# Second FF product by seven quarter products: three sweeps in place of two, and stores on GpSimd's queue

## The chip, the core and the metric

One NeuronCore of a Trainium2 chip runs the whole program. The metric is the device time of one execution in microseconds (us). Three runs of the kernel before gave 828.68, 830.63 and 832.57 us, a median of 830.63. Engines are named TensorE (PE, with PEld for its weight loads), VectorE (DVE), ScalarE (ACT), GpSimd (POOL) and SyncE (SP, which only issues DMAs here).

## The reference, cut to what matters

The program is a decoder block for 512 tokens of width 1024 in float32: gated attention and convolution mixers, a projection with norm and residual, and then a squared-ReLU MLP. The change touches the last part alone:

```python
def squared_relu_mlp(h, w_ff1, w_ff2):
    return jnp.square(jax.nn.relu(h @ w_ff1)) @ w_ff2
...
    f = squared_relu_mlp(rms_norm(x, norm_mlp_pre[l]), w_ff1[l], w_ff2[l])
    x = x + rms_norm(f, norm_mlp_post[l])
```

Here h is 512 x 1024, w_ff1 is 1024 x 4096 and w_ff2 is 4096 x 1024.

## The kernel before, in words

Every float32 operand of a matmul is split into a high part (a cast to float32r on ScalarE) and a low part (the difference, on VectorE), and `mm3` (lines 84 to 88) issues three matmuls per product: high x high, high x low, low x high. A matmul has a 128x128 stationary block and 512 moving columns.

The first FF product works through 32 blocks j of 128 FF channels. `wsplit` (99) loads a block's weights in two halves into `raw` buffers (tag `raw`, six of them, `NRAW`), casts them into `whi` and subtracts into `wlo` (four each), and `ff1_part` (685) runs 24 matmuls into a PSUM bank. `ff1_end` (694) takes the ReLU on ScalarE and the product with the bank on VectorE; the result, FF channels by tokens, stays in `f1`. Two blocks, j = 2p and 2p + 1, make a pair p; there are 16 pairs (`NP`).

The second FF product sums, over the pairs, products of 2 x 2 blocks: the rows are the lower and the upper token half (256 tokens), the columns of w_ff2 are its two halves of 512, and the inner index is the pair's two blocks. Instead of eight quarter products it takes seven (Strassen's scheme in Winograd's form), of two token tiles and three matmuls each: 42 matmuls for a pair. PSUM has eight banks of 128x512, and a quarter product needs two for as long as it is summed over the pairs, so the seven are made in two sweeps over the pairs. The names in the code: a for the quarters of `f1`, b for those of w_ff2, s and t for sums of them.

- The first sweep runs along with the first FF product. For each pair `first_operands` (737) loads the four quarters of w_ff2 (`quarter`, 720, into `raw` buffers), forms the sums s2, s3, t3, t2, t4, splits them, and overwrites quarters of `f1` with the sums that the second sweep needs. `first_sweep` (757) of pair p - 1 follows, three quarter products in six banks, 18 matmuls: s3 t3, s2 t2, a22 t4.
- The second sweep has four quarter products (`second_operands`, 762; `second_products`, 779), 24 matmuls for a pair. It loads all four quarters of w_ff2 again, forms t1 again and splits the whole of `f1[p]`. The first product of pair 0 is placed ahead of the last step of the first sweep, since two banks are free by then.
- The end (834 to 854) takes the last two pairs (`TAIL`) token tile by token tile and product by product. As banks are completed, VectorE combines them into output tiles: tiles 2 and 3 (lower half) from products 0 and 1 and the sums `g` and `h` of the first sweep, tiles 0 and 1 from products 2 and 3 and `e`. `post` (827) takes the mean square (`square_sums`, 643: ScalarE squares with a sum, GpSimd adds and raises to -0.5), multiplies by the gain, adds the residual and stores (`finish`, 820), all stores on SP's queue.

Who goes when: the program is written in order, but a planner of the language sets the order on each engine and queue beforehand, by its own estimates of costs and by the program's order as priority; a tile is given one of its tag's buffers when one is free. On the chip each engine works its list in order and waits where an operand or a buffer is not ready. SP's list holds the loads and, before the change, the output stores.

Of the kernel before, what the change touches and what calls it, by code (L numbers as in the profile page):

```python
# [11 lines left out]
F32 = mybir.dt.float32  # L12
F32R = mybir.dt.float32r
# [6 lines left out]
P = 128  # L20
# [26 lines left out]
NRAW = 6  # L47
# [11 lines left out]
def decoder_block(ctx: ExitStack, tc: tile.TileContext, a: dict, out: bass.AP):  # L59
# [15 lines left out]
    def stile(name, dt=F32):  # L75
        return spool.tile([P, 512], dt, tag="s", name=name, bufs=6)
# [657 lines left out]
    def htile(name, dt=F32R):  # L734
        return hpool.tile([P, 4, S], dt, tag="h", name=name, bufs=4)

    def first_operands(p):

        f = f1[p]
        b12, b22, b11, b21 = (quarter(2 * p + r, c) for r, c in ((0, 1), (1, 1), (0, 0), (1, 0)))  # L740
        w = [htile(f"x{x}{p}") for x in "hl"]
        s23 = stile(f"s23{p}")
        a22 = stile(f"a22{p}", F32R)
        split(a22[:, half[0]], a22[:, half[1]], f[:, 1, half[1]])
        dve.tensor_tensor(s23[:, half[1]], f[:, 0, half[0]], f[:, 0, half[1]], ALU.subtract)
        dve.tensor_tensor(f[:, 0, half[1]], f[:, 0, half[1]], f[:, 1, half[1]], ALU.add)
        dve.tensor_tensor(s23[:, half[0]], f[:, 0, half[1]], f[:, 0, half[0]], ALU.subtract)
        split(w[0][:, 3, :], w[1][:, 3, :], s23)
        ts = [stile(f"t{n}{p}") for n in (3, 2, 4)]
# [12 lines left out]
    def second_operands(p):  # L762

        b12, b11, b21, b22 = (quarter(2 * p + r, c, *t) for r, c, *t in (
            (0, 1, "whi", NSPLIT), (0, 0), (1, 0), (1, 1)))
        t1 = stage.tile([P, 512], F32, tag="wlo", name=f"t1{p}", bufs=NSPLIT)
        l = htile(f"l{p}")
        w = [r3.tile([P, 4, 512], F32R, tag="sw", name=f"y{x}{p}", bufs=4) for x in "hl"]
        split(l[:, 0:2, :], l[:, 2:4, :], f1[p])
        split(w[0][:, 0, :], w[1][:, 0, :], b11)  # L770
        dve.tensor_tensor(t1, b12, b11, ALU.subtract)
        for n, src in ((1, t1), (2, b21), (3, b22)):
            split(w[0][:, n, :], w[1][:, n, :], src)
        return l, w


    LEFT = ((0, 0), (0, 1), (1, 0), (1, 1))

    def second_products(p, ops, which, toks=(0, 1)):
        l, w = ops  # L780
        for n in which:
            r, c = LEFT[n]
            products(bcc[n], [l[:, r, half[c]], l[:, 2 + r, half[c]]], [x[:, n, :] for x in w], p == 0, p == NP - 1, toks)

    ops = {}
    for p in range(NP):
        for j in (2 * p, 2 * p + 1):
            if j < BRIDGE:
                pf, w = early[j]
                ff1_part(pf, w, SPLIT, S)  # L790
            else:
                w = wsplit(a["w_ff1"][j], f"f1{j}", eng=dve)
                pf = ps(f"pf{j}")
                ff1_part(pf, w, 0, S)
            ff1_end(j, pf)
        ops[p] = first_operands(p)
        if p == 1:
            acc = [[scs(f"p70"), scs("p71")], [cvtile("p60"), cvtile("p61")], [tps("p40"), ps("p41")]]
        if p:
            first_sweep(p - 1, ops.pop(p - 1))  # L800
    gout = gain("g_out", a["norm_mlp_post"], D)
    second = second_operands(0)
    bcc = [[ps(f"p1{t}") for t in range(2)]]
    second_products(0, second, (0,))
    first_sweep(NP - 1, ops.pop(NP - 1))

    e, g = (ratile(n) for n in ("e", "g"))
    h = wtile("h")
    for t in range(2):
        act.copy(e[:, t, :], acc[1][t])  # L810
        dve.tensor_tensor(g[:, t, :], acc[0][t], e[:, t, :], ALU.add)
        dve.tensor_tensor(h[:, t, :], g[:, t, :], acc[2][t], ALU.subtract)
    bcc += [[cvtile(f"p5{t}") for t in range(2)], [scs(f"p2{t}") for t in range(2)], [tps("p30"), ps("p31")]]
    second_products(0, second, (1, 2, 3))
    for p in range(1, NP - TAIL):
        second_products(p, second_operands(p), range(4))

    o_ = [wtile(f"o{t}") for t in range(NT)]

    def finish(t, r):  # L820
        for c, n in ((0, 512), (512, 512)) if t != 1 else ((0, 512), (512, 256), (768, 256)):
            hf, c1 = divmod(c, 512)
            piece = o_[t][:, hf, c1:c1 + n]
            dve.scalar_tensor_tensor(piece, piece, r, x1[t][hf][:, c1:c1 + n], ALU.mult, ALU.add)  # L824
            sp.dma_start(out[t * P:(t + 1) * P, c:c + n], piece)

    def post(t):
        src = [o_[t][:, hf, :] for hf in range(2)]
        r = square_sums(src, f"o{t}")
        for hf in range(2):  # L830
            dve.tensor_tensor(src[hf], src[hf], gout[:, hf * 512:(hf + 1) * 512], ALU.mult)  # L831
        finish(t, r)

    last = [(p, second_operands(p)) for p in range(NP - TAIL, NP)]
    for t in range(2):
        v = stile(f"v{t}")
        for n in (0, 1, 2, 3):
            for p, x in last:
                second_products(p, x, (n,), (t,))
            bank = bcc[n][t]  # L840
            if n == 0:
                act.copy(v, bank)
                dve.tensor_tensor(o_[t + 2][:, 0, :], v, h[:, t, :], ALU.add)
            elif n == 1:
                dve.tensor_tensor(g[:, t, :], g[:, t, :], bank, ALU.add)
                dve.tensor_tensor(e[:, t, :], e[:, t, :], bank, ALU.add)  # L846
                dve.tensor_tensor(o_[t + 2][:, 1, :], g[:, t, :], v, ALU.add)
                post(t + 2)
                pool.tensor_tensor(e[:, t, :], e[:, t, :], v, ALU.add)  # L849
            elif n == 2:  # L850
                dve.tensor_tensor(o_[t][:, 0, :], v, bank, ALU.add)
            else:
                dve.tensor_tensor(o_[t][:, 1, :], e[:, t, :], bank, ALU.add)
                post(t)


def _layout(i):
# [58 lines left out]
```

## Time and profile before

| | before |
|---|---|
| median of three runs | 830.63 us |
| the profiled execution | 830.19 us, of which its span 828.4 |
| TensorE busy | 797.4 us, 96% of the span |
| VectorE, ScalarE, GpSimd busy | 633.0, 419.7, 215.6 us |
| TensorE's granted clock, mean | 0.991 of full |
| DMA queue of SP and the other hardware queues, GpSimd's | 94.09 and 1.57 MB |
| bytes read from and written to HBM | 93.54 and 2.10 MB |

The profile is of one execution. Times in it count from the start of the span. "Busy" sums the instructions of an engine; a matmul's shown end is modelled, and matmuls overlap, so that one with 0.40 us shown can be followed by the next after 0.23. In a timeline an arrow names what ended the idle time before an instruction. SPq and POOLq are the instructions that issue a DMA on these engines' queues; the time to landing counts from the issue until all bytes are there.

### The profile page before, as it was taken

The numbers are of one execution on the slowest core, as the hardware profiler recorded it, in microseconds if no ns is written. First come the engines' busy times: TensorE is split into PE (matmuls) and PEld (weight loads), VectorE is DVE, ScalarE is ACT, GpSimd is POOL, SyncE is SP. The second block draws the span as 40 slices with busy tenths as digits, with TensorE's granted clock in tenths as the row PEclk, the third lists the DMA queues.
The fourth block names the chain that finished last, engine by engine and source line by source line (L and its number), as shares of the span: only waits on it lengthen the run. The fifth ranks groups of instructions, "written<-read, shape, count | busy, mean of one in ns | idle before, by whom it ended". The sixth has DMA issues, their size and how long they took to land. (4 is left out here: it accounts for less than half of the span.)

```text
span 828.4 us, 11002 instructions
## 1 busy us (share of the span) xinstructions
PE 797.4 (96%) x3786; PEld 660.7 (80%) x3786; DVE 633.0 (76%) x1046; ACT 419.7 (51%) x792; POOL 215.6 (26%) x203
## 2 busy tenths in 40 slices
PE   8989999999999999899999999999999999999992
PEld 8967888888888887687878898888888888788871
DVE  5689999999999996596573547857657657798777
ACT  6667775867673233365442324434334334555642
POOL 3244433433434645648711100000000000000003
PEclk9999999999999999999999999999999999999997
DMA  8412121122112223245450014544434334466422
GB/s 265 137 41 90 52 80 51 53 80 70 68 62 100 91 101 104 89 162 188 159 191 1 27 49 155 178 135 144 141 127 153 128 127 165 154 210 202 157 67 101
DMA packets 54344, 96.36 MB, mean 116 GB/s; under 512 B 6288, under 2 KB 11280, under 8 KB 54288
## 3 DMA queue, kind: packets, MB, share of 16 engines
q1 hardware_dynamic: 53856, 94.09, 34.1%
q0 software_dynamic: 432, 1.57, 0.5%
q8 instruction: 30, 0.49, 0.3%
q14 instruction: 26, 0.21, 0.1%
HBM read 93.54 MB, written 2.10 MB: 115 GB/s over the span
## 5 line engine op out<-in xcount | busy, mean ns | idle before, releaser
L559 DVE SCALAR_TENSOR_TENSOR cv<-u,convw,cv 128x512 f32<-128x512 f32 x232 | 161.9, 747 | 0.2
L87 PE MATMUL pf<-h2l,whi_f 128*128 128x512 f32 (+1 forms) x256 | 97.4, 380 | 0.0
L86 PE MATMUL pf<-h2h,whi_f 128*128 128x512 f32 (+1 forms) x256 | 97.3, 380 | 0.0
L88 PE MATMUL pf<-h2h,wlo_f 128*128 128x512 f32 (+1 forms) x256 | 97.3, 381 | 0.0
L112 DVE TENSOR_TENSOR wlo_f<-raw_f,whi_f 128x512 fp32r<-128x512 f32 x60 | 41.1, 690 | 65.1 <-ACT whi_f L111 63.9
L849 POOL TENSOR_TENSOR e<-e,v 128x512 f32<-128x512 f32 x2 | 3.2, 1600 | 329.4 <-DVE e L846 329.4
L111 ACT CAST whi_f<-raw_f 128x512 fp32r<-128x512 f32 x60 | 36.9, 621 | 85.0 <-PE pf L87 50.0
L112 POOL TENSOR_TENSOR wlo_gt<-raw_gt,whi_gt 128x512 fp32r<-128x512 f32 x32 | 43.9, 1374 | 50.1 <-ACT whi_gt L111 50.1
L87 PEld LDWEIGHTS pf<-h2l,whi_f 128*128 128x128 f32 x256 | 48.2, 188 | 9.9
L86 PEld LDWEIGHTS pf<-h2h,whi_f 128*128 128x128 f32 x256 | 48.2, 188 | 9.9
L88 PEld LDWEIGHTS pf<-h2h,wlo_f 128*128 128x128 f32 x256 | 48.2, 188 | 9.8
L86 PE MATMUL pg<-hTh,whi_gt 128*128 128x512 f32 x128 | 51.4, 402 | 0.0
L88 PE MATMUL pg<-hTh,wlo_gt 128*128 128x512 f32 x128 | 50.6, 396 | 0.0
L87 PE MATMUL pg<-hTl,whi_gt 128*128 128x512 f32 x128 | 50.5, 395 | 0.0
L86 PE MATMUL p<-yh,l 128*128 128x512 f32 x128 | 50.4, 395 | 0.0
L87 PE MATMUL p<-yl,l 128*128 128x512 f32 x128 | 50.4, 395 | 0.0
L88 PE MATMUL p<-yh,l 128*128 128x512 f32 x128 | 50.2, 395 | 0.0
L726 ACT CAST yh<-f 128x512 fp32r<-128x512 f32 x48 | 28.0, 617 | 36.8 <-PE p L87 27.6
L727 DVE TENSOR_TENSOR yl<-f,yh 128x512 fp32r<-128x512 f32 x48 | 31.7, 687 | 14.8 <-ACT yh L726 14.7
L111 ACT CAST whi_gt<-raw_gt 128x512 fp32r<-128x512 f32 x32 | 19.8, 618 | 40.1 <-PE pg L87 37.0
L726 ACT CAST xh<-t 128x512 fp32r<-128x512 f32 x48 | 29.6, 619 | 19.5 <-DVE t L751 19.5
L727 DVE TENSOR_TENSOR xl<-t,xh 128x512 fp32r<-128x512 f32 x48 | 31.5, 684 | 0.5 <-ACT xh L726 0.5
(314 smaller groups left out, 2278.6 us busy)
## 6 DMA issues: line engine op xcount, KB each, us to landing
f<-in_w_ff SPq DMA_DIRECT2D x128, 256.0 KB, 3.0
raw_f<-in_w_ff SPq DMA_DIRECT2D x64, 256.0 KB, 3.0
raw_gt<-in_w_zm SPq DMA_DIRECT2D x32, 256.0 KB, 2.5
raw_gb<-in_w_zm SPq DMA_DIRECT2D x16, 256.0 KB, 2.6
raw_ga<-in_w_zm SPq DMA_DIRECT2D x16, 256.0 KB, 2.6
raw_wo<-in_w_o SPq DMA_DIRECT2D x16, 256.0 KB, 2.6
raw_pw<-in_w_pw SPq DMA_DIRECT2D x16, 256.0 KB, 2.7
raw_wout<-in_w_out SPq DMA_DIRECT2D x16, 256.0 KB, 2.7
```

The source lines that it names most:

```text
L86: pe.matmul(o, lhsT=lh, rhs=rh, start=first, stop=False)
L87: pe.matmul(o, lhsT=lh, rhs=rl, start=False, stop=False)
L88: return pe.matmul(o, lhsT=ll, rhs=rh, start=False, stop=last)
L111: recent[act] = act.copy(hi, raw)
L112: recent[e] = e.tensor_tensor(lo, raw, f32(hi), ALU.subtract)
L559: dve.scalar_tensor_tensor(co[j] if tap == CW - 1 else acc[j], src, convw[:, i, tap:tap + 1], acc[j], ALU.mult, ALU.add)
L726: act.copy(hi, src)
L727: dve.tensor_tensor(lo, src, f32(hi), ALU.subtract)
L849: pool.tensor_tensor(e[:, t, :], e[:, t, :], v, ALU.add)
```

## The change

- The seven products are made in three sweeps. The first, still along with the first FF product, has a11 b11, s2 t2 and s3 t3. The second has two products that complete the lower token half (they read the upper columns of `f1[p]`, and t1 and t4). The third has two that complete the upper half (with b21 and b22 raw from w_ff2).
- t1 and t4 are formed in the first sweep, in place in the `raw` buffers of b12 and b21, and stored to DRAM (`keep`), 32 stores of 256 KB on GpSimd's queue; the second sweep loads them back into `whi` and `raw` buffers instead of two quarters of w_ff2.
- `later_operands` splits half of `f1[p]` (512 columns) for each of the later sweeps, and two right operands.
- Ahead of the first sweep's last step stand the first products of pairs 0 and 1 of the second sweep.
- `lower` is a generator of 14 steps that finishes output tiles 2 and 3; one step is taken behind each pair 0 to 13 of the third sweep. Their stores go to GpSimd's queue, those of tiles 0 and 1 stay on SP's.
- The last two pairs of the third sweep are taken token tile by token tile, as before, with two products each; one VectorE addition completes an output half.

```diff
+    def keep(name, p, src):
+        kept[name, p] = dram.tile([P, 512], F32, tag=f"{name}{p}", name=f"{name}{p}")
+        pool.dma_start(kept[name, p], src)
...
     def first_operands(p):
...
-        a22 = stile(f"a22{p}", F32R)
-        split(a22[:, half[0]], a22[:, half[1]], f[:, 1, half[1]])
+        a11 = stile(f"a11{p}", F32R)
+        split(a11[:, half[0]], a11[:, half[1]], f[:, 0, half[0]])
+        split(w[0][:, 0, :], w[1][:, 0, :], b11)
...
-        ts = [stile(f"t{n}{p}") for n in (3, 2, 4)]
-        for n, (t, x, y, op) in enumerate(((ts[0], b22, b12, ALU.subtract), (ts[1], ts[0], b11, ALU.add), (ts[2], ts[1], b21, ALU.subtract))):
-            dve.tensor_tensor(t, x, y, op)
-            split(w[0][:, n, :], w[1][:, n, :], t)
-        dve.tensor_tensor(f[:, 1, half[1]], f[:, 1, half[0]], s23[:, half[0]], ALU.subtract)
+        t3, t2 = (stile(f"t{n}{p}") for n in (3, 2))
+        dve.tensor_tensor(t3, b22, b12, ALU.subtract)
+        dve.tensor_tensor(t2, t3, b11, ALU.add)
+        split(w[0][:, 2, :], w[1][:, 2, :], t3)
+        split(w[0][:, 1, :], w[1][:, 1, :], t2)
+        dve.tensor_tensor(b12, b12, b11, ALU.subtract)
+        keep("t1", p, b12)
+        dve.tensor_tensor(b21, t2, b21, ALU.subtract)
+        keep("t4", p, b21)
+        dve.tensor_tensor(f[:, 0, half[0]], f[:, 1, half[0]], s23[:, half[0]], ALU.subtract)
         s2, s3 = ([x[:, 3, h] for x in w] for h in half)
-        return (s3, s2, [a22[:, h] for h in half]), w
+        return ([a11[:, h] for h in half], s2, s3), w
...
+    def later_operands(p, beta):
+
+        if beta:
+            raw = [quarter(2 * p + 1, c) for c in range(2)]
+        else:
+            raw = []
+            for n, (tag, bufs) in (("t1", ("whi", NSPLIT)), ("t4", ("raw", NRAW))):
+                raw.append(stage.tile([P, 512], F32, tag=tag, name=f"{n}b{p}", bufs=bufs))
+                sp.dma_start(raw[-1], kept[n, p])
...
+        w = r3.tile([P, 4, 512], F32R, tag="sw", name=f"y{beta}{p}", bufs=4)
+        split(l[:, 0:2, :], l[:, 2:4, :], f1[p][:, :, half[1 - beta]])
+        for n in range(2):
+            split(w[:, n, :], w[:, 2 + n, :], raw[n])
         return l, w
...
+    ahead = [later_operands(p, 0) for p in range(2)]
+    bcc = [[ps(f"p5{t}") for t in range(2)]]
+    for p in range(2):
+        later_products(p, 0, ahead[p], (0,))
     first_sweep(NP - 1, ops.pop(NP - 1))
...
+    for t in range(2):
+        act.copy(u1[:, t, :], acc[0][t])
+    for t in range(2):
+        dve.tensor_tensor(u2[:, t, :], acc[1][t], u1[:, t, :], ALU.add)
+        dve.tensor_tensor(u3[:, t, :], acc[2][t], u2[:, t, :], ALU.add)
...
+    for p in range(2):
+        later_products(p, 0, ahead[p], (1,))
+    for p in range(2, NP):
+        later_products(p, 0, later_operands(p, 0))
...
+            (sp if t < 2 else pool).dma_start(out[t * P:(t + 1) * P, c:c + n], piece)
+            yield
...
+    def lower():
+        for t in range(2):
+            yield from post(t + 2, (
+                lambda: dve.tensor_tensor(o_[t + 2][:, 0, :], u3[:, t, :], bcc[1][t], ALU.subtract),
+                lambda: dve.tensor_tensor(o_[t + 2][:, 1, :], u3[:, t, :], bcc[0][t], ALU.add),
+                lambda: dve.tensor_tensor(u2[:, t, :], u2[:, t, :], bcc[0][t], ALU.add)))
+
+    rest = lower()
+    for p in range(NP - TAIL):
+        later_products(p, 1, later_operands(p, 1))
+        next(rest, None)
+    last = [(p, later_operands(p, 1)) for p in range(NP - TAIL, NP)]
+    for _ in rest:
+        pass
+    upper = [post(t, ()) for t in range(2)]
     for t in range(2):
+        for n, src in ((0, u1), (1, u2)):
             for p, x in last:
+                later_products(p, 1, x, (n,), (t,))
+            dve.tensor_tensor(o_[t][:, n, :], src[:, t, :], bcc[2 + n][t], ALU.add)
+            if t and n == 0:
+                next(upper[0])
+                next(upper[0])
+    for u in upper:
+        for _ in u:
+            pass
```

## Rows read from the trace of the kernel before

**Rows 1.** Page, part 1: busy us (share) xinstructions of each engine

```profile
PE 797.4 (96%) x3786; PEld 660.7 (80%) x3786; DVE 633.0 (76%) x1046; ACT 419.7 (51%) x792; POOL 215.6 (26%) x203
```

**Rows 2.** Stretches: us; busy PE, PEld, DVE, ACT, POOL; PEclk, DMA share, GB/s

```profile
670.00:700.00 30.00, 30.00 (x131) 24.39 (x131) 19.17 (x37) 12.32 (x22) 0.00 (x0) 1.00 0.41 140
700.00:720.00 20.00, 18.02 (x79) 14.35 (x78) 14.13 (x27) 9.68 (x18) 0.00 (x0) 1.00 0.60 198
740.00:760.00 20.00, 20.00 (x87) 16.11 (x86) 17.71 (x25) 11.58 (x19) 0.00 (x0) 1.00 0.63 208
800.00:828.40 28.40, 12.10 (x52) 9.20 (x50) 22.38 (x33) 9.01 (x22) 8.20 (x10) 0.79 0.20 74
```

**Rows 3.** Timeline at the seam: start, duration, instruction, [idle before it <-releaser]

```profile
712.65 0.69 DVE L699 TENSOR_TENSOR f<-pf,rl 128x512 f32<-128x512 f32 x1 [1.15 <-ACT rl L696]
...
715.65 0.40 PE L88 MATMUL p<-xh,a 128*128 128x512 f32 x1
...
715.80 0.62 ACT L726 CAST yh<-f 128x512 fp32r<-128x512 f32 x1 [1.72 <-DMA f<-in_w_ff]
...
716.33 1.13 ACT L726 CAST xh<-t 128x512 fp32r<-128x512 f32 x2
...
718.03 0.73 PE L86 MATMUL p<-xh 128*128 128x512 f32 x2 [1.98 <-ACT xh L726]
```

**Rows 4.** Timeline of the tail

```profile
811.70 0.40 PE L88 MATMUL p<-yh,l 128*128 128x512 f32 x1
...
820.62 0.67 DVE L853 TENSOR_TENSOR o<-e,p 128x512 f32<-128x512 f32 x1
...
821.38 0.63 ACT L647 ACTIVATE j_o<-o 128x512 bf16<-128x512 f32 x1 [1.80 <-DVE o L853]
...
823.08 0.56 POOL L145 TENSOR_TENSOR r_o<-v_o,mhalf 128x1 f32<-128x1 f32 x1
...
823.67 1.54 DVE L824 SCALAR_TENSOR_TENSOR o<-o,r_o,x 128x512 f32<-128x512 f32 x3 [0.85 <-POOL r_o L145]
```

**Rows 5.** Groups by shape, 720 to 800: busy us, mean ns | idle

```profile
L727 DVE TENSOR_TENSOR l<-f,l 128x1024 fp32r<-128x1024 f32 x16 | 19.5, 1222 | 0.1
...
L771 DVE TENSOR_TENSOR t<-f,f 128x512 f32<-128x512 f32 x15 | 10.3, 685 | 1.9 <-DMA f<-in_w_ff 1.8
```

**Rows 6.** Timeline of pairs 0 and 1 in the first sweep

```profile
493.46 0.42 DVE L745 TENSOR_TENSOR s<-f 128x256 f32<-128x256 f32 x1
...
495.07 0.68 DVE L751 TENSOR_TENSOR t<-t,f 128x512 f32<-128x512 f32 x1
...
495.78 7.08 SPq L104 DMA_DIRECT2D raw_f<-in_w_ff  x4
...
498.84 0.62 ACT L111 CAST whi_f<-raw_f 128x512 fp32r<-128x512 f32 x1 [0.26 <-DMA raw_f<-in_w_ff]
...
499.02 0.42 DVE L753 TENSOR_TENSOR f<-f,s 128x256 f32<-128x256 f32 x1
...
500.55 0.68 DVE L112 TENSOR_TENSOR wlo_f<-raw_f,whi_f 128x512 fp32r<-128x512 f32 x1
...
501.94 0.39 PE L86 MATMUL pf<-h2h,whi_f 128*128 128x512 f32 x1
```

**Rows 7.** DMA issues: xcount, KB each, median us from issue to landing

```profile
f<-in_w_ff SPq DMA_DIRECT2D x128, 256.0 KB, 3.0
...
out<-o SPq DMA_DIRECT2D x7, 256.0 KB, 2.0
...
g_out<-in_norm_mlp_post POOLq DMA_DIRECT2D x1, 512.0 KB, 4.0
```

**Rows 8.** Timeline of POOL: the last DMA issue on its queue

```profile
475.86 0.64 POOL L140 DMA_DIRECT2D g_out<-in_norm_mlp_post  x1
```

**Rows 9.** Timeline at block 30: first cast of its weights, first use

```profile
689.42 0.62 ACT L111 CAST whi_f<-raw_f 128x512 fp32r<-128x512 f32 x1 [2.34 <-DMA raw_f<-in_w_ff]
...
700.61 0.39 PE L86 MATMUL pf<-h2h,whi_f 128*128 128x512 f32 x1
```

More of the change, by code (lines that the diff above doesn't have):

```diff
@@ L735, in htile @@
         return hpool.tile([P, 4, S], dt, tag="h", name=name, bufs=4)
+    dram = open_pool(ctx, "dram", bass.MemoryType.DRAM)
+    kept = {}
+    def keep(name, p, src):
+        kept[name, p] = dram.tile([P, 512], F32, tag=f"{name}{p}", name=f"{name}{p}")
+        pool.dma_start(kept[name, p], src)
     def first_operands(p):
@@ L760, in first_sweep, with later_products @@
             products(bank, l, [x[:, n, :] for x in w], p == 0, p == NP - 1)
[L762 to L773, printed above, removed]
+    lpair = [None]
+    def later_operands(p, beta):
[6 more added lines that the diff above has]
+                sp.dma_start(raw[-1], kept[n, p])
+        if not beta and p < 2:
+            l = rapool.tile([P, 4, 2 * P], F32R, tag="ra", name=f"l{beta}{p}", bufs=4)
+        else:
+            if p % 2 == 0:
+                lpair[0] = hpool.tile([P, 8, 2 * P], F32R, tag="h", name=f"l{beta}{p}", bufs=4)
+            l = lpair[0][:, 4 * (p % 2):4 * (p % 2) + 4, :]
+        w = r3.tile([P, 4, 512], F32R, tag="sw", name=f"y{beta}{p}", bufs=4)
+        split(l[:, 0:2, :], l[:, 2:4, :], f1[p][:, :, half[1 - beta]])
+        for n in range(2):
+            split(w[:, n, :], w[:, 2 + n, :], raw[n])
         return l, w
-    LEFT = ((0, 0), (0, 1), (1, 0), (1, 1))
-    def second_products(p, ops, which, toks=(0, 1)):
+    def later_products(p, beta, ops, which=(0, 1), toks=(0, 1)):
         l, w = ops
         for n in which:
-            r, c = LEFT[n]
-            products(bcc[n], [l[:, r, half[c]], l[:, 2 + r, half[c]]], [x[:, n, :] for x in w], p == 0, p == NP - 1, toks)
+            r = 1 - n if beta else n
+            products(bcc[2 * beta + n], [l[:, r, :], l[:, 2 + r, :]], [w[:, n, :], w[:, 2 + n, :]],
+                     p == 0, p == NP - 1, toks)
     ops = {}
@@ L797, in decoder_block @@
         if p == 1:
-            acc = [[scs(f"p70"), scs("p71")], [cvtile("p60"), cvtile("p61")], [tps("p40"), ps("p41")]]
+            acc = [[scs("p10"), scs("p11")], [cvtile("p60"), cvtile("p61")], [tps("p70"), ps("p71")]]
         if p:
@@ L801, in decoder_block, with post @@
     gout = gain("g_out", a["norm_mlp_post"], D)
-    second = second_operands(0)
-    bcc = [[ps(f"p1{t}") for t in range(2)]]
-    second_products(0, second, (0,))
+    ahead = [later_operands(p, 0) for p in range(2)]
+    bcc = [[ps(f"p5{t}") for t in range(2)]]
+    for p in range(2):
+        later_products(p, 0, ahead[p], (0,))
     first_sweep(NP - 1, ops.pop(NP - 1))
-    e, g = (ratile(n) for n in ("e", "g"))
-    h = wtile("h")
+    u12, u3 = htile("u12", F32), htile("u3", F32)
+    u1, u2 = u12[:, 0:2, :], u12[:, 2:4, :]
     for t in range(2):
[L810 to L816, printed above, removed]
-    o_ = [wtile(f"o{t}") for t in range(NT)]
-    def finish(t, r):
+        act.copy(u1[:, t, :], acc[0][t])
+    for t in range(2):
+        dve.tensor_tensor(u2[:, t, :], acc[1][t], u1[:, t, :], ALU.add)
+        dve.tensor_tensor(u3[:, t, :], acc[2][t], u2[:, t, :], ALU.add)
+    bcc += [[f(f"{n}{t}") for t in range(2)] for f, n in ((scs, "p4"), (cvtile, "p2"))] + [[tps("p30"), ps("p31")]]
+    for p in range(2):
+        later_products(p, 0, ahead[p], (1,))
+    for p in range(2, NP):
+        later_products(p, 0, later_operands(p, 0))
+    o_ = [wtile(f"o{t}") for t in range(NT)]
+    def post(t, combine):
+        src = [o_[t][:, hf, :] for hf in range(2)]
+        for c in combine:
+            c()
+            yield
+        r = square_sums(src, f"o{t}")
+        for hf in range(2):
+            dve.tensor_tensor(src[hf], src[hf], gout[:, hf * 512:(hf + 1) * 512], ALU.mult)
+            yield
         for c, n in ((0, 512), (512, 512)) if t != 1 else ((0, 512), (512, 256), (768, 256)):
@@ L824, in finish @@
             dve.scalar_tensor_tensor(piece, piece, r, x1[t][hf][:, c1:c1 + n], ALU.mult, ALU.add)
[L825 to L834, printed above, removed]
+            (sp if t < 2 else pool).dma_start(out[t * P:(t + 1) * P, c:c + n], piece)
@@ new lines, in post @@
+            yield
+    def lower():
[8 more added lines that the diff above has]
+        next(rest, None)
@@ L835, in decoder_block @@
+    last = [(p, later_operands(p, 1)) for p in range(NP - TAIL, NP)]
+    for _ in rest:
+        pass
+    upper = [post(t, ()) for t in range(2)]
     for t in range(2):
-        v = stile(f"v{t}")
-        for n in (0, 1, 2, 3):
+        for n, src in ((0, u1), (1, u2)):
             for p, x in last:
[L839 to L854, printed above, removed]
+                later_products(p, 1, x, (n,), (t,))
[3 more added lines that the diff above has]
+                next(upper[0])
```

## The prediction

> **What bounds the kernel now.** I read the page's first part, then the busy time by stretches, then the timeline at the two places where TensorE is not full. TensorE is busy for 797.4 of the 828.4 us span [rows 1]. By stretches it is full (30.00 of 30) in the first sweep and full in the second, at a granted clock of 1.00, with 87 matmuls in 20 us, or 0.230 us each; it loses 2 us around 716 and most of the stretch after 800 [rows 2]. So a saving can come from three things only: fewer matmuls, the gap at the seam between the sweeps, or the tail. The matmuls stay the same: 7 products of 6 matmuls per pair of FF blocks, 42, before and after (18 + 24 now, 18 + 12 + 12 then).
>
> The seam [rows 3]: the last matmul of sweep 14 starts at 715.65, and the next, the first of pair 15, at 718.03, after 1.98 us idle. It waited for ScalarE's cast of t3. ScalarE could not make it: the cast ahead of it in its queue, an operand of the second sweep, sat until 715.80 for a load of w_ff2 (1.72 us idle). The casts that TensorE needed followed at 716.33.
>
> The tail [rows 4]: the last matmul starts at 811.70 and takes 0.40, so TensorE ends at 812.10 and the span 16.3 us later. VectorE then works off both halves of token tile t=1: combinations, squares, gains, residuals, stores. The last combination starts only at 820.62, and what follows it is a chain to the end: ScalarE's square (821.38), GpSimd's power (823.08), the three residual pieces (823.67 to 825.21), the store and the end of the program at 828.4, 7.78 us in all.
>
> **The change, part by part.**
>
> *Tail.* The four lower output halves are finished during the third sweep: 14 steps of one VectorE instruction, one behind each of the pairs 0 to 13. After the last matmul there is one combination of t=1 (I allow 0.1 us between them), then the same chain of 7.78 us. In that chain VectorE also has two residual pieces of t=0 (1.4) and two gain products (1.3); with the combination these 3.4 us fit before GpSimd's power, due 3.0 us after the combination began, almost exactly. So 7.9 us in place of 16.3: **-8.4 us**. If the planner puts t=0's two pieces ahead of the last combination, 1.5 us come back; below 7.8 it cannot go.
>
> What hides the 14 steps: a pair in the third sweep takes TensorE 12 x 0.230 = 2.76 us. VectorE has one half-width left operand (512 columns, 0.69 by the 512-column row; the full one takes 1.222), two low parts (2 x 0.69) and the step (0.69) [rows 5], 2.74 us. That looks like no margin, but back to back such instructions start every 0.60 us (seven of 512 and four of 256 columns start between 493.46 and 499.02) [rows 6], so 2.4 us, and operands lie up to four pairs ahead (four `sw` buffers). I take zero, with 1 us as the upper end. The first step waits for the last bank of the second sweep; behind it on VectorE wait the operands of pair 1, for which there are 2.76 us and 2.4 are needed: zero.
>
> *Seam.* Sweep 15 now begins with a11 b11, which needs neither t3 nor s3, and the second sweep's filler ahead of it is 12 matmuls instead of 6 (pairs 0 and 1, from kept tiles). After the first matmul block ends, TensorE has sweep 14 (18), the filler (12) and a11 b11 (6): 36 x 0.230 = 8.3 us, to about 720.2. The operands of s2 t2 follow f (712.65 to 713.34) by two half sums, two sums, three casts and low parts, some 4 us, thus by 717.5. The wait goes: **-2.0 us**. Late next would be the left operand of pair 2, whose buffer comes free when sweep 15 ends; the n=1 products of pairs 0 and 1 (12, 2.76 us) cover its cast and low part (1.3) and VectorE's two u3 sums (1.3). Bounds: -2.2 to 0.
>
> *Loads and stores.* The second and third sweep load two quarters each per pair, four together as now; in the third all use the six `raw` buffers, three pairs or 8.3 us deep, against a load of 3.0 us [rows 7] and some 2 us of cast and subtraction: zero. New are 32 stores of 256 KB during the first sweep. On GpSimd, busy 0.00 there [rows 2], one issue takes 0.64 us [rows 8], so 20 us on an idle engine; behind them on its queue is nothing that TensorE needs. On the DMA engines the stores add two transfers to eight per pair: 0.41 of their time [rows 2] becomes about 0.51, less than the 0.63 that the second sweep bears. VectorE gets one more 512-column instruction per pair, 0.6 us in 15.3, at 19.17 of 30 busy: zero. On SP's queue, which keeps loads alone, nothing stands between a load and a store any more.
>
> *The price: raw buffers held by the stores.* t1 and t4 are formed in place in two of the six `raw` buffers, and these come free only when their stores have landed. Now the buffers come free when the sums are done. In the first pairs that is tight [rows 6]: SP issues the first load for block 4 at 495.78, as the second sum (started 495.07) ends; its cast starts at 498.84 (3.06 later), its low part at 500.55, and TensorE uses it at 501.94, with nothing else to do by about 502.0, when sweep 0 is through. In the new order the first buffer goes to a quarter of pair 1, the second too, and this load takes the third: t1's, after its store. By VectorE's order t1 ends where the old chain had its eleventh instruction, about 499.0 if all follow f; three that don't need it (low parts of a11 and b11, half of s23) can run ahead, so I take 497.75. A store: between 2.0 us (256 KB from SP's queue) and 4.0 (512 KB on GpSimd's) [rows 7]; I take 3.0. So the load issues at 500.75, its cast starts at 503.8, its low part is ready 1.3 later at 505.1, and the third matmul, due at 502.4, waits: **+2.75 us**. Ends: zero, if t1 goes ahead of the casts and the store takes 2.0; +6, with t1 at 499.0, 4.0 for the store and the low part behind VectorE's work on pair 1 as now (1.7 from cast to low part).
>
> A page puts this price a little lower: the Trainium skill, DMA: Bandwidth & Descriptors, section Anatomy of one DMA, fits a GpSimd-issued transfer by 2.0 us plus bytes over 436 GB/s, an estimated 2.6 us for 256 KB; the sum below would be 0.4 us lower. No run here shows a store on that queue yet.
>
> Later pairs hide the same delay. The first cast for block 30 is made at 689.42 and first used at 700.61 [rows 9]: with 1.35 for cast and low part, 9.8 us of slack. The shift is 500.75 - 495.78 = 5.0 us.
>
> **Sum.** -8.4 - 2.0 + 2.75 = -7.65 us. The profiled execution took 830.19 (span 828.4 and 1.8 around it): 822.5. It lies 0.44 under the median of 830.63, so against that 823.0, which I give.
>
> **Rivals.**
>
> A. *No stall at block 4* (t1 early and its store quick). For: the quarters of pair 0 are loaded long before. Against: in the old kernel too the sums of pair 0 ran only among those on f [rows 6], and the planner had no other work for TensorE. 830.63 - 10.4 = 820.2.
>
> B. *It does not do what it says: the lower half is not hidden.* The order on each engine is the planner's, by its own costs, and the seam shows it placing a cast ahead of a load that was late [rows 3]. If it puts most of the 14 steps behind the third sweep, the tail keeps its 16.3 us, and only the seam is won and the stall paid: 830.63 - 2.0 + 2.75 = 831.4. Against: the steps are written between the pairs, and are ready there.
>
> C. *Slower: the stores starve the first sweep.* Place: the same buffers, but in every pair from 2 to 15. If a store takes over 3.0 + 4.8 = 7.8 us to land, the slack is used up, and each further us costs 1 us in each of 14 pairs. From 8.7 us on the kernel is slower in sum than by the bound below; at 9.0 the pairs cost 16.8 us and block 4 another 8.75: 830.63 - 10.4 + 25.5 = 845.7. For: VectorE is 64% busy there, and GpSimd has to write the descriptors beside it. Against: the one issue on GpSimd's queue beside VectorE's work took 0.64 us [rows 8]. This is what a rule would do that speaks against the move: the Trainium skill, SBUF — State Buffer, section SBUF: two separate sides, has descriptor writing for such a queue locked out while VectorE runs in a two-port mode, and advises the other queues. The same page, Who interferes with whom, excepts the two-input additions and subtractions that VectorE runs here, as an inference; the one issue in [rows 8] fits that.
>
> **How the numbers follow.** A measurement of this kernel can tell about 0.5%, 4.15 us, from no change. Forecast 0.45, A 0.25, B 0.17, C 0.13. The forecast's own ends: stall 0 to 6, seam up to 2 less, tail up to 1.5 less, so 819.6 to 829; A reaches to 818 with the runs' scatter. The range 817.5 to 829 holds forecast and A with the nearer part of B. Faster (under 826.5) are A and nearly all of the forecast, 0.70; within 0.5% is B and the forecast's far end, 0.18; slower is C, 0.12.
>
> **What would show it.** Right: TensorE without a gap between 711 and 725; after its last matmul some 8 us; the first cast for block 4 waiting for a load behind t1's store, TensorE idle 1 to 5 us near 502, and nowhere else in the first sweep; GpSimd's stores landing in 2 to 4 us; VectorE near 85 to 90% busy in the third sweep, TensorE full. Wrong: TensorE idle once per pair (C), residual pieces of t=2 and 3 after the last matmul (B), or TensorE waiting for VectorE's low parts in the third sweep, which I cost at zero.

## The result, and the profile after

The change made the kernel **slower**: 851.33 us median of four runs (849.58 to 854.25), against 830.44 for four runs of the kernel before on the same chip. The ratio is 1.0254, interval 1.0216 to 1.0292. 823.0 was forecast. The profiled execution took 849.58 us, its span 847.8, that is 19.4 us over the span of before. By stages (starts of the first matmul on `pm`, line 86, and of the last on `pf`, line 88, then TensorE's end):

| | before | after | difference | forecast |
|---|---|---|---|---|
| first matmul of `pm` | 425.5 | 428.3 | +2.7 | 0 |
| from there to the last of `pf` | 286.0 | 309.2 | +23.2 | +2.75 |
| to TensorE's end | 100.6 | 101.6 | +1.0 | -2.0 |
| to the span's end | 16.3 | 8.8 | -7.5 | -8.4 |

(Differences are taken before rounding.) The first row belongs to work whose lists of instructions are the same in both kernels; the other versions of the new kernel below start there at 427 to 430 too. 1.0 us of it is there by 70 us, and 1.2 more comes between 344 and 356, where the granted clock was 0.79 (341 to 357) against 0.89 in before (340 to 356). What set that I leave open. The loss is the second row.

First the page of after (its first part, and a line of its DMA issues, with the median us from issue to landing at the end); the first line answers to [rows 1]:

```profile
PE 809.5 (95%) x3786; PEld 665.9 (79%) x3786; DVE 630.7 (74%) x1060; ACT 419.2 (49%) x806; POOL 231.7 (27%) x237
...
t<-f POOLq DMA_DIRECT2D x32, 256.0 KB, 3.9
```

By stretches of after (columns as in [rows 2]; answers of several queries):

```profile
610.00:640.00 30.00, 27.74 (x119) 21.83 (x118) 18.47 (x36) 9.92 (x18) 2.16 (x4) 1.00 0.49 167
...
670.00:700.00 30.00, 27.51 (x112) 21.87 (x112) 20.54 (x38) 11.49 (x21) 2.16 (x4) 0.94 0.42 141
...
760.00:820.00 60.00, 60.00 (x259) 48.27 (x258) 49.54 (x80) 39.29 (x76) 4.25 (x7) 1.00 0.56 188
```

TensorE was full in every stretch of the first sweep; now it lacks 2 to 2.5 us in 30, and in the stretch of 670 to 700 the granted clock is 0.94. From 760 on, through the third sweep, it is full. The waits of TensorE between 500 and 760 (us in total, times, longest) show where:

```profile
PE pf L88 <- DVE wlo_f L112: 14.9, 11, 2.5
PE p L86 <- DVE f L699: 1.4, 1, 1.4
PE p L86 <- ACT xh L726: 1.1, 2, 0.9
PE pf L86 <- ACT whi_f L111: 0.7, 1, 0.7
PE p L88 <- DVE l L727: 0.6, 1, 0.6
```

In the kernel before, the same view has one wait, the 2.0 us at the seam. Now the first FF product waits for the low part of its weights, nearly once per pair. The step from one pair to the next was 15.27 us; from 571 to 726 it is now 17.2 in the mean.

One such turn, two steps of it, in the timeline of after. L762 is t1, L764 t4, L742 their stores, the SPq rows L722 loads of quarters of w_ff2, the SPq rows L104 loads of FF weights:

```profile
609.94 0.69 DVE L762 TENSOR_TENSOR f<-f,f 128x512 f32<-128x512 f32 x1
...
610.92 1.14 POOL L742 DMA_DIRECT2D t<-f  x2 [15.36 <-DVE f L762]
...
614.53 6.82 SPq L104 DMA_DIRECT2D raw_f<-in_w_ff  x4
...
617.29 0.62 ACT L726 CAST xh<-f 128x512 fp32r<-128x512 f32 x1 [5.86 <-DMA f<-in_w_ff]
...
618.63 0.62 ACT L111 CAST whi_f<-raw_f 128x512 fp32r<-128x512 f32 x1 [0.72 <-DMA raw_f<-in_w_ff]
...
619.65 0.62 ACT L111 CAST whi_f<-raw_f 128x512 fp32r<-128x512 f32 x1 [0.40 <-DMA raw_f<-in_w_ff]
620.18 0.59 ACT L696 ACTIVATE rl<-pf 128x512 f32<-128x512 f32 x1
...
621.25 0.68 DVE L699 TENSOR_TENSOR f<-pf,rl 128x512 f32<-128x512 f32 x1
622.52 0.68 DVE L758 TENSOR_TENSOR t<-f,f 128x512 f32<-128x512 f32 x1
...
626.88 0.69 DVE L762 TENSOR_TENSOR f<-f,f 128x512 f32<-128x512 f32 x1
...
627.86 1.14 POOL L742 DMA_DIRECT2D t<-f  x2 [15.80 <-DVE f L762]
629.16 0.50 PE L88 MATMUL pf<-h2h,wlo_f 128*128 128x512 f32 x1 [1.32 <-DVE wlo_f L112]
```

It is a **loop**. t1 ends; its store is issued at 610.92; 3.61 us later, when the buffer is free, the next pair's weight load is issued at 614.53. ScalarE's list has the cast of b11 and two weight casts ahead of the ReLU: the second of them waits for that load (0.72), the third for the next (0.40), and the ReLU (620.18) stands behind them without idle time of its own. Behind it, in the order of VectorE's list, come f (621.25), t3 (622.52) and, 4.36 us later behind t2 and three low parts, the next t1 (626.88), after which it begins anew. From t3 to t3 that is 16.6 us (605.91, in the same view, to 622.52), and TensorE needs only 15.27. Nine such turns, from 571.42 to 725.93, took 16.4 to 18.3 us, 17.2 in the mean; in the longest a weight cast ahead of t3's waits for its load as well (2.35 us at 642.00), and t1 comes 6.0 us behind t3.

t4 is in the loop too: the second weight load (issued at 617.06) waited for t4's store. The trace has t1's stores landing 3.5 us after their issue at the median and t4's, issued some 0.6 us behind them, 5.3. And t1 frees a third buffer, since it now is the last reader of b11. The waits of SP's list between 500 and 740 (us in total, times, longest) show both, quarters of w_ff2 waiting for t1 and FF weights for stores:

```profile
SPq L722 <- DVE f L762: 51.5, 13, 5.6
SPq L104 <- DMA t<-f: 40.5, 25, 3.3
```

What of the 23.2 us that is: 13 waits in the first sweep with 16.5 us of idle time (14.9 + 0.9 + 0.7); about 0.27 each beyond the idle shown, by the spacing of the matmul starts around a wait, 3.5; and two stretches at a lower clock, 3.2 (last section). Sum 23.2.

The seam of after, beside [rows 3]: that wait is gone, and three smaller ones have come. In the chain of waits (start, us, what) it is the last pairs' stores that are late, since t1 and t4 are loaded again at once; the last block's ReLU (742.61) stands on ScalarE behind casts of t1 and t4 that waited for these loads:

```profile
731.75 5.35 DMA t<-f
...
737.12 4.07 DMA t4b<-t
...
741.21 0.63 ACT y L726
...
741.87 0.70 DVE y L727
...
742.58 3.77 DMA t4b<-t
```

The tail of after, beside [rows 4]:

```profile
838.63 0.40 PE L88 MATMUL p<-y,l 128*128 128x512 f32 x1
...
839.53 0.68 DVE L879 TENSOR_TENSOR o<-u,p 128x512 f32<-128x512 f32 x1
...
840.25 0.63 ACT L647 ACTIVATE j_o<-o 128x512 bf16<-128x512 f32 x1 [1.08 <-DVE o L879]
...
841.07 1.10 POOL L649 TENSOR_SCALAR v_o<-ss_o 128x1 f32<-128x1 f32 x1 [2.31 <-ACT j_o L647]
842.25 0.56 POOL L145 TENSOR_TENSOR r_o<-v_o,mhalf 128x1 f32<-128x1 f32 x1
842.84 1.54 DVE L856 SCALAR_TENSOR_TENSOR o<-o,r_o,x 128x512 f32<-128x512 f32 x3 [0.76 <-POOL r_o L145]
```

One combination after the last matmul (ended 839.03), then the chain, as forecast: 8.8 us where 16.3 had been.

### The profile page after: what moved, and what is told of

It is laid out like the page before. It is cut to its first block, busy times and chain, and to the rows that moved or that the text cites. A ratio compares the mean times of both kernels' runs of the same rounds, so it can differ in the third digit from the quotient of the medians.

```text
span 847.8 us, 11143 instructions
## 1 busy us (share of the span) xinstructions
PE 809.5 (95%) x3786; PEld 665.9 (79%) x3786; DVE 630.7 (74%) x1060; ACT 419.2 (49%) x806; POOL 231.7 (27%) x237
## 4 chain that ended last, share of the span: by engine, by line
issue 23%; PE 17%; DVE 4%; DMA 3%; POOL 2%; ACT 1%; POOLq 0%; DVEq 0%; ACTq 0%
PE p L88 3%; PE p L86 3%; PE p L87 3%; PE pm L88 2%; POOL t L742 2%; PE pm L87 2%; PE pm L86 2%; DMA t<-f 1%; DMA t4b<-t 1%; DVE xl L727 1%; PE pf L88 1%; PE pf L86 1%; PE pf L87 1%; DMA f<-in_w_ff 1%; PE pth L681 0%
## 5 line engine op out<-in xcount | busy, mean ns | idle before, releaser
L88 PE MATMUL pf<-h2h,wlo_f 128*128 128x512 f32 (+1 forms) x256 | 99.6, 391 | 14.9 <-DVE wlo_f L112 14.9
L87 PE MATMUL pf<-h2l,whi_f 128*128 128x512 f32 (+1 forms) x256 | 98.5, 385 | 0.0
L742 POOL DMA_DIRECT2D t<-f x32 | 17.4, 543 | 252.1 <-DVE f L762 251.2
L727 DVE TENSOR_TENSOR xl<-f,xh 128x512 fp32r<-128x512 f32 x16 | 11.1, 692 | 55.7 <-ACT xh L726 55.7
L86 PE MATMUL p<-y,l 128*128 128x512 f32 x128 | 50.6, 396 | 1.4 <-DVE f L699 1.4
L88 PE MATMUL p<-y,l 128*128 128x512 f32 x128 | 50.6, 396 | 0.6 <-DVE l L727 0.6
L87 PE MATMUL p<-y,l 128*128 128x512 f32 x128 | 50.5, 395 | 0.0
L726 ACT CAST xh<-f 128x512 fp32r<-128x512 f32 x16 | 9.9, 620 | 74.4 <-DMA f<-in_w_ff 73.6
L696 ACT ACTIVATE rl<-pf 128x512 f32<-128x512 f32 x32 | 19.0, 594 | 26.8 <-PE pf L88 26.8
L727 DVE TENSOR_TENSOR xl<-t,xh 128x512 fp32r<-128x512 f32 x32 | 21.7, 687 | 12.6 <-ACT xh L726 12.6
```

The source lines that it names most:

```text
L86: pe.matmul(o, lhsT=lh, rhs=rh, start=first, stop=False)
L87: pe.matmul(o, lhsT=lh, rhs=rl, start=False, stop=False)
L88: return pe.matmul(o, lhsT=ll, rhs=rh, start=False, stop=last)
L696: act.activation(rl, pf, AF.Relu)
L742: pool.dma_start(kept[name, p], src)
```

## The experiments

Three theories went in. **H**, the held buffers: t1 and t4, formed in place in `raw` buffers, keep these from the loads. **Q**, an order on ScalarE: b11's cast, new ahead of the ReLU, waits for its own load. **D**, the stores themselves: their share of the DMA engines, or of GpSimd. All runs are set against the kernel before on the same chip: 834.44 (one run) for the first four, 832.33 (eleven) for the next four, 830.63 (eleven) for the last four. These differ by up to 4 us from chip to chip, so versions are compared by their distance from their own before (after: 20.9 us above), or by the first sweep. "First sweep" below is the second row of the table, 286.0 before and 309.2 after. Where no number of runs is given, it is one.

**e1: t1 and t4 into a tile of their own.**

```diff
-        dve.tensor_tensor(b12, b12, b11, ALU.subtract)
-        keep("t1", p, b12)
-        dve.tensor_tensor(b21, t2, b21, ALU.subtract)
-        keep("t4", p, b21)
+        t14 = ratile(f"t14{p}")
+        dve.tensor_tensor(t14[:, 0, :], b12, b11, ALU.subtract)
+        keep("t1", p, t14[:, 0, :])
+        dve.tensor_tensor(t14[:, 1, :], t2, b21, ALU.subtract)
+        keep("t4", p, t14[:, 1, :])
```

> Theories. H: the kernel after is slow because t1 and t4 are formed in place, so that two of the six raw buffers are held until their stores land, and the loads of the next weights start late. Q: it is slow because the cast of b11 was put ahead of the ReLU on ScalarE's list and waits there for its load, whatever the stores do. D: it is slow because of the 32 stores themselves, their share of the DMA engines or GpSimd's work on their descriptors beside VectorE. This kernel forms t1 and t4 in buffers of another tag that lie free in this stage (tag ra), so a raw buffer is free as soon as the sum is made; stores, their queue and the place of b11's cast in the program stay. H: 820 to 826 us, ScalarE's waits for loads ahead of b11's cast under 20 us instead of 73.6. Q: over 840. D: 847 to 855.

825.26 us; first sweep 287.4. All but 1.4 us of the loss is gone, and 32 stores of the same size run on the same queue. H, and not D. Nor Q as the cause by itself: b11's cast still stands ahead of the ReLU, and ScalarE's waits for its load come to 16.4 us in place of 73.6 (480 to 745).

**e2: b11's cast tied behind t3's.**

```diff
-        split(w[0][:, 0, :], w[1][:, 0, :], b11)
...
+        cast = act.copy(w[0][:, 2, :], t3)
+        with tc.issue_after(cast.ins):
+            act.copy(w[0][:, 0, :], b11)
```

> The kernel after with one thing changed: b11's cast is tied behind t3's cast on ScalarE, so it no longer stands ahead of the ReLU of the pair's second block; stores hold raw buffers as in the kernel after. Q: 820 to 830 us. H: 843 to 853, the weights' casts still wait for loads that wait for stores. D: 847 to 855.

860.23, slower still, and above every range given. With the cast no longer ahead of the ReLU the loss stays, so Q falls. The edit did more than it was to do: b11's cast and low part now stand ahead of t1, which comes 5.12 us behind t3 (625.18 to 630.30), so buffers are held longer, and TensorE's waits for `wlo_f` grow to 18.6 us. The cast is a place where the loop can be seen, not what drives it.

**e3: no stores.** t1 and t4 are formed in place and not kept; the second sweep loads quarters of w_ff2 in their place, so it computes other products.

```diff
-        pool.dma_start(kept[name, p], src)
...
-                sp.dma_start(raw[-1], kept[n, p])
+                sp.dma_start(raw[-1], a["w_ff2"][2 * p][:, 512 * (n == "t4"):512 * (n == "t4") + 512])
```

> The kernel after without the 32 stores; the second sweep loads quarters of w_ff2 in place of t1 and t4, so its products are of other numbers (the lower half of the output is not the reference's), with the same transfers and instructions otherwise. H and D: 818 to 824 us, TensorE without a gap once per pair. Q: over 835, since b11's cast stands where it did.

836.48; first sweep 294.4. By the letter this lies in Q's range and outside that of H and D; but e1 and e2 speak against Q, and what H's range left out is that a buffer is held until t1 is formed even when nothing is stored. Of the 21.8 us between the first sweeps of after and e1, 14.8 go with the stores and their landing (309.2 - 294.4), and 7.0 with forming in place alone. SP's list still waits for t1 (500 to 740):

```profile
SPq L722 <- DVE f L761: 44.7, 14, 3.3
```

The two parts are not cleanly apart, for in this version the planner puts the casts in another order (the ReLU waits behind a third weight cast, itself 3.23 us late for its load at 631.72), so what of the 7.0 us is due to that order stays open.

**e4: in place, stores on SP's queue.**

```diff
-        pool.dma_start(kept[name, p], src)
+        sp.dma_start(kept[name, p], src)
```

> The kernel after with the stores of t1 and t4 issued on SP's queue between the loads, as the output stores of the kernel before were. Landing should be 2 us in place of 3.9. H: a store that lands 1.9 us earlier frees the buffer as much earlier, most of the 1.7 us that a pair lasts too long: 825 to 840, less if SP's list now waits for VectorE's sums ahead of loads. D, if by GpSimd's descriptors: 820 to 828; if by the DMA engines' share: 847 to 855. Q: 845 to 855.

837.14; first sweep 296.9. The stores land sooner (its DMA issues, and TensorE's waits between 480 and 745):

```profile
t<-f SPq DMA_DIRECT2D x32, 256.0 KB, 2.1
```

```profile
PE pf L88 <- DVE wlo_f L112: 6.5, 10, 1.7
```

The loop, from one t3 to the next, is 617.62 to 633.39, 15.8 us (16.1 in the mean of nine turns): 0.5 over what TensorE needs, and its ten waits come to 6.5 us. With the sums in place, a separate queue for the stores was the slower choice of the two.

**e5: e1 again, with more runs** (the edit of e1).

> The kernel of e1 (t1 and t4 formed in ra buffers, everything else of the change kept), timed in rounds. One look gave 825.26 against 834.44 of the kernel before on that chip, a ratio of 0.989. H: 0.985 to 0.993, faster; D and Q: no gain, 0.998 or more, the one look being chance.

826.75 (824.62 to 827.46, six runs), ratio to before 0.9927, interval 0.9909 to 0.9944: 0.7% below the kernel before, small but clear of the scatter, and well below after (ratio 1.0254). The same stretch of a pair in its timeline:

```profile
611.94 0.68 DVE L699 TENSOR_TENSOR f<-pf,rl 128x512 f32<-128x512 f32 x1
613.21 0.68 DVE L758 TENSOR_TENSOR t<-f,f 128x512 f32<-128x512 f32 x1
...
614.15 0.68 DVE L759 TENSOR_TENSOR t<-t,f 128x512 f32<-128x512 f32 x1
614.86 7.45 SPq L104 DMA_DIRECT2D raw_f<-in_w_ff  x4
...
618.43 0.68 DVE L763 TENSOR_TENSOR t<-f,f 128x512 f32<-128x512 f32 x1
```

The weight loads are issued 1.65 us after t3 begins, right behind t2 (L759, the last reader of b11's buffer). In after it was 8.62 (605.91 to 614.53). t1 (L763) no longer writes over an operand of t3, so it need not follow it: here, at 618.43, it is the next pair's. Before the change the distance was 1.99 (622.33 to 624.32).

**e6: in place, but t1 and t4 formed right behind t2**, ahead of the casts and low parts.

```diff
         dve.tensor_tensor(t2, t3, b11, ALU.add)
+        dve.tensor_tensor(b12, b12, b11, ALU.subtract)
+        keep("t1", p, b12)
+        dve.tensor_tensor(b21, t2, b21, ALU.subtract)
+        keep("t4", p, b21)
         split(w[0][:, 2, :], w[1][:, 2, :], t3)
...
-        dve.tensor_tensor(b12, b12, b11, ALU.subtract)
-        keep("t1", p, b12)
-        dve.tensor_tensor(b21, t2, b21, ALU.subtract)
-        keep("t4", p, b21)
```

> The kernel after with one thing moved: t1 and t4 are formed, in place as there, right behind t2 and ahead of the low parts of s23, t3 and t2, so their stores start some 1.8 us earlier in each pair. H: a pair that lasts 1.65 us too long gets most of that back, 826 to 842. Q and D: unchanged, 845 to 858, since the stores and the order on ScalarE stay.

833.56; first sweep 293.1. The buffers are held for a store as before, but t1 begins 1.54 us after t3 in place of 4.36, and from 580 on nothing is lost:

```profile
500.00:580.00 80.00, 75.71 (x317) 59.94 (x316) 53.56 (x99) 29.80 (x55) 5.40 (x10) 0.98 0.53 173
580.00:720.00 140.00, 140.00 (x604) 113.00 (x603) 95.70 (x173) 56.44 (x102) 9.71 (x18) 1.00 0.53 176
```

A turn is 615.57 to 630.92, 15.35 us, and here TensorE sets it: e5, in pairs without a wait, steps by 15.35 too, and the ReLU behind the two casts now waits for TensorE and not for a load:

```profile
613.66 0.60 ACT L696 ACTIVATE rl<-pf 128x512 f32<-128x512 f32 x1 [0.81 <-PE pf L88]
```

So the way round is shorter than a pair; by how much the trace does not say. The same held buffers cost something once, in the first pairs, when that way is no longer than a pair, and in every pair when it is longer. Of after, e4 and e6, in which the ReLU stands behind the same two casts, a turn takes 17.2, 16.1 and 15.3 us in the mean of nine, and the first sweep is 23.2, 10.9 and 7.1 us above before's.

**e7: e1 with its stores on SP's queue** (the edits of e1 and e4).

> The kernel of e1 with the stores of t1 and t4 on SP's queue between the loads, instead of GpSimd's: what the separate queue is worth once no raw buffer waits for a store. H: the queue matters only by SP's waits for VectorE's sums ahead of loads; within 4 us of e5 either way. D, if GpSimd's descriptors cost VectorE time: 3 us or more faster than e5. If the separate queue is what lets the loads run: 5 us or more slower.

824.26, a single run, 2.5 us under e5's median on the same chip. The queue that the change moved the stores to gives nothing; SP's own serves as well. That it serves better is not shown: e9, six runs with it, is not to be told from e5.

**e8: e1 without the interleaving**: the 14 steps of the lower half stand behind pair 13 of the third sweep in the program, not between its pairs.

```diff
         later_products(p, 1, later_operands(p, 1))
-        next(rest, None)
```

> The kernel of e1 without the steps between the pairs of the third sweep: all 14 steps of the lower half stand behind the operands of the last two pairs, ahead of the upper half's combinations. That is rival B made by hand. If the interleaving hides them, as the prediction costs at zero: 14 steps of 0.6 us and two waits for GpSimd's power stand in front of the last combinations, beside 24 matmuls of the last two pairs (5.5 us): 3 to 8 us slower than e5. If VectorE is the limit of the third sweep: within 2 us of e5.

826.25, within e5's runs, as expected if VectorE were the limit of the third sweep; but the reason is another. The planner runs the steps early all the same: first and last of the lower half's on VectorE in e8 (L865 a combination, L857 a residual piece):

```profile
770.05 0.68 DVE L865 TENSOR_TENSOR o<-u,p 128x512 f32<-128x512 f32 x1
...
797.93 0.74 DVE L857 SCALAR_TENSOR_TENSOR o<-o,r_o,x 128x512 f32<-128x512 f32 x1
```

What shortens the tail is that the lower half's products are complete a sweep earlier, not where its steps are written.

**e9: e7 with the left operand of pairs 2 and 3 given its buffer ahead of `u3`**, against the wait of 1.4 to 1.5 us for `l` at the seam that e1, e5 and e8 have (TensorE's waits of e5, between 480 and 745):

```profile
PE p L86 <- ACT l L726: 1.5, 1, 1.5
PE pf L88 <- DVE wlo_f L112: 0.9, 1, 0.9
```

```diff
-    u12, u3 = htile("u12", F32), htile("u3", F32)
+    u12 = htile("u12", F32)
+    lpair[0] = hpool.tile([P, 8, 2 * P], F32R, tag="h", name="l02", bufs=4)
+    u3 = htile("u3", F32)
```

> t1 and t4 in a tile of their own, their stores on SP's queue, and the left operand of pairs 2 and 3 given its buffer ahead of u3, so that the seam's wait for the cast of l (1.4 to 1.5 us in the four versions with the own tile) can go. If the seam's wait is TensorE's alone and nothing else is late behind it: 1.4 us under the version without that edit, 822.9 from its one look of 824.26. If the buffer is given no earlier, or the next operand is late by as much: no change, 824.3. If the stores on SP's queue only looked quicker by chance: 825.3, that is 1.4 under the 826.75 of the version with GpSimd's queue.

825.95 (824.42 to 827.35, six runs), ratio to before 0.9938, interval 0.9918 to 0.9957; not to be told from e5. In its profile the wait is 0.3, but e7, without this edit, has 0.3 there too (the expectation counted it among those with 1.4), so it was the move to SP's queue, and not the edit, that removed it. Of the three expectations the last came nearest, but the 1.4 us under e5 that it rests on do not show against the kernel before (4.7 us below it here, 5.6 in e5).

**Which of the two, t1 or t4?** One at a time in a tile of its own, first t1:

```diff
-        dve.tensor_tensor(b12, b12, b11, ALU.subtract)
-        keep("t1", p, b12)
+        t1 = ratile(f"t1{p}")
+        dve.tensor_tensor(t1[:, 0, :], b12, b11, ALU.subtract)
+        keep("t1", p, t1[:, 0, :])
```

> Only t1 leaves the raw buffers, t4 stays in place in b21's. Theory of the held buffers, with t1 as the late one (b12 came free at t3 before, and b21 at t4 as in place too, so that t4 in place adds only its store's landing): most of the loss goes, 828 to 833. Rival, the landing of the stores alone, two equal halves: 838 to 840, half way between 826.75 and 851.33. Rival, DMA traffic or GpSimd's queue: unchanged, about 851.

827.55 us, a single run, 3.1 below its before; first sweep 289.1, against 287.4 to 287.7 in e1, e5 and e8. With t1 out of the way, t4 in place costs 1.4 to 1.7 us: t1 is the one that must follow t3, which reads b12, and that is placed late. t4 stands where the chain of the old kernel also ended the use of b21; its store holds one buffer longer, and that is covered.

Then t4:

```diff
-        dve.tensor_tensor(b21, t2, b21, ALU.subtract)
-        keep("t4", p, b21)
+        t4 = ratile(f"t4{p}")
+        dve.tensor_tensor(t4[:, 0, :], t2, b21, ALU.subtract)
+        keep("t4", p, t4[:, 0, :])
```

> Only t4 leaves the raw buffers, t1 stays in place in b12's, which holds b12 and b11 until t1 is formed. Theory of the held buffers, with t1 as the late one: most of the loss stays, 842 to 850. Rival, the landing of the stores alone: 838 to 840. Rival, DMA traffic or GpSimd's queue: unchanged, about 851.

858.11, a single run: the loss stays, as expected, but it came out 27.5 us above its before, 6.6 more than after, and outside the range given. 3.4 of these lie in the first sweep (312.6), most of the rest behind it. Its loop in one pair is 642.66 to 659.94, 17.3 us, with a third weight cast ahead of the ReLU; that the planner's order changed with the tile is all I can say.

**e10: the kernel before with five `raw` buffers.** Is a shorter ring by itself the price?

```diff
-NRAW = 6
+NRAW = 5
```

> The kernel before with five raw buffers in place of six. If a shorter ring by itself is the price of the change: slower by 10 us or more, TensorE waiting once in every pair of the first sweep. If the ring has slack in the kernel before and only the way back from t1 to the loads repeats the delay: within 4 us of the kernel before, a stall at the first pairs at most.

843.95, but not where the change lost. The first matmul of `pf` starts at 484.4 in place of 474.0 (10.5 us later, unrounded), in stages ahead of it that load through the same buffers; from there to the last of `pf` it is 240.5, against 237.6, 2.9 more. TensorE's waits in it between 480 and 745:

```profile
PE p L86 <- ACT xh L726: 2.0, 1, 2.0
PE pf L88 <- DVE wlo_f L112: 1.1, 3, 0.5
```

A buffer fewer throughout costs the first sweep 3 us. That bears out the slack I had read there [rows 9], and that one buffer fewer does not explain 23. Two fewer, or the new kernel with more of them, were not run.

## Why the prediction was wrong

- **Tail, -8.4: right.** 8.8 us after the last matmul where 7.9 was reckoned; of the 0.9 between, 0.4 lies ahead of the combination (839.53 - 839.03 = 0.5, and I had allowed 0.1), 0.3 in the chain from there to the residual pieces (839.53 to 842.84, 3.31, and 3.05 in [rows 4]), 0.2 behind them.
- **The 14 steps cost nothing: right**, TensorE was full from 760 to 820, with VectorE 83% busy where 85 to 90 had been reckoned. Rival B did not happen, and e8 shows that it could not have come from the place of the steps in the program.
- **Seam, -2.0: the old wait went, as reckoned, and 2.2 us of new ones came** (1.40 + 0.27 + 0.57). I named the left operand of pair 2 as late next; the stores of the last pairs, which have to land before t1 and t4 are loaded back, were later. I had not followed them. In e9, with these waits down to 0.3, the stage is 98.5 us, 2.1 under before's.
- **Stall at block 4, +2.75: right in kind, its size in part luck.** TensorE waited 0.73 us for block 4's weights (509.20) and 0.86 for the cast of s (506.50), which I had not priced; with 0.27 beyond each, 2.1 us. Set against f of pair 0, which comes 2.2 us later in after than before (495.02, 492.86), the load behind t1's store was issued 1.2 us later than I had it (504.09 for 500.75). It cost no more because nine more matmuls, 2.1 us, stand ahead of that block than in the kernel before (27 of the sweep in place of 18), which I had not reckoned.
- **The step that failed: "Later pairs hide the same delay."** I set a shift of 5.0 us against a slack of 9.8 and took the slack as a stock that is there again in each pair. The shift came out at 6.6 (8.62 - 1.99), still under 9.8, and yet TensorE waited in nearly every pair. Slack between a cast and its use says how late a load may be once. Here the late load holds up ScalarE's list, ScalarE holds the ReLU, that holds f, f holds t3 and t1 behind it on VectorE's list, and t1 holds the next load. What counts is the loop's length against TensorE's 15.27 us: 17.2 in the mean of after. The term that I had put at nothing, later pairs, cost some 21 of the 23.2 us.
- **Rival C named the place and the buffers, but put its decision point too far off**: a store over 7.8 us, from the same slack. Stores of 3.5 (t1) and 5.3 us (t4) were enough. (By C's own terms the kernel is slower from 8.3 us on, not 8.7: 14 x 0.47 + 8.0 is already the 10.4 won plus the bound of 4.15.) C was given a chance of 0.13. It also counted only the store; t1's wait for t3 and its place behind three low parts made up more of the way (4.36 us from t3 to t1, 3.61 from the store's issue to the load's).
- **The store's price, 3.0 with ends 2.0 and 4.0:** measured 3.9 at the median of all 32 (3.5 for t1's, 5.3 for t4's), and 2.1 on SP's queue (e4). The nearest row was the 4.0 of a GpSimd transfer; I averaged it with another queue's. The Trainium skill, DMA: Bandwidth & Descriptors, section Anatomy of one DMA, which would give an estimated 2.6 for it, is lower than the measurement, and the measurement decides. GpSimd's time was right: 32 issues at 0.54 us each in after (17.4 us in all), with VectorE busy through all of them, below the 0.64 of [rows 8]. The Trainium skill, SBUF — State Buffer, section Who interferes with whom, excepts two-input additions and subtractions from what locks GpSimd out of writing descriptors, as an inference; that no issue grew agrees with it. Why the stores land later on this queue than on SP's no run here tells.
- **Every forecast stage but one was within 3.0 us.** With that loop removed (e5) the kernel takes 826.75, a gain of 5.6 over its own before, of the 7.65 I had summed.

## What to carry to other kernels

When a result is written in place into a buffer of a load ring, ask what its last reader is, where the writer stands in its engine's list, and when the store lands; then add up the whole way round to the same instruction of the next iteration, over every in-order list on it. If the sum is below the bound engine's time for an iteration, the delay is paid once; if it is above, the difference is paid each time, however much slack one edge shows. A tile of its own for a result that outlives its operands takes it out of the loop (e5); forming it directly behind the last read made the loop shorter than a pair here, at 7.1 us paid once (e6).

## What the runs showed of the hardware

Two of after's waits cost TensorE more than their length. The stretches around the two longest, of 2.49 us each, the second of them in single matmuls:

```profile
647.00:651.00 4.00, 3.73 (x10) 2.97 (x11) 1.41 (x3) 0.00 (x0) 0.11 (x1) 0.62 0.86 278
...
682.00:686.00 4.00, 3.77 (x10) 3.00 (x11) 1.38 (x3) 0.00 (x0) 0.08 (x1) 0.57 0.86 292
```

```profile
682.24 0.80 PE L88 MATMUL pf<-h2h,wlo_f 128*128 128x512 f32 x1 [2.49 <-DVE wlo_f L112]
682.83 0.63 PE L86 MATMUL pf<-h2h,whi_f 128*128 128x512 f32 x1
683.25 0.63 PE L87 MATMUL pf<-h2l,whi_f 128*128 128x512 f32 x1
683.68 0.63 PE L88 MATMUL pf<-h2h,wlo_f 128*128 128x512 f32 x1
```

After each, TensorE ran for some 3 us with 0.43 us from matmul to matmul in place of 0.23, that is at the lower of its two levels, 1.2 GHz in place of 2.4; by the granted clocks of 0.62 and 0.57 the two stretches cost 0.38 x 4 + 0.43 x 4 = 3.2 us. The other eleven waits in after's first sweep, of 0.23 to 1.85 us, were followed by no such stretch. The length of a wait alone does not tell, though: in e6 one of 1.83 us (543.66) was, with a granted clock of 0.75 from 545 to 550.

And a 256 KB store from SBUF to DRAM landed 3.9 us (after) and 3.5 us (e5) after its issue on GpSimd's queue, 2.1 us (e4) and 2.2 us (e7) on SP's, at the median of 32. Of two stores issued 0.6 us apart on GpSimd's queue in after the first took 3.5 us and the second 5.3; on SP's queue in e4, 2.0 and 2.2.
